# A decoder layer on one core: the first step's way down begun one chunk later, a cast put behind copies, and cached keys asked for ahead of raw weights

## The chip, the cores and the metric

The kernel runs on one core of one Trainium2 chip. The metric is the device time of one execution in microseconds; three runs of the kernel before gave 1118.55 us as their median (1118.25 to 1120.14). The engines are TensorE (PE, matrix products), VectorE (DVE), ScalarE (ACT), GpSimd (POOL) and SyncE (SP), which here issues most of the DMAs. Each engine works through its own queue, and semaphores hold an instruction until what it needs is done.

## The reference

One layer is applied to 576 rows: 512 of a prompt and 8 sample sequences of 8. The width is 1024, the hidden width of an FFN 2816, everything in float32. Cut to what matters:

```
x = x + 0.5 * swiglu(rmsnorm(x), ffn1...)          # silu(x@w_gate) * (x@w_up) @ w_down
h = rmsnorm(x); u_lru, gate, u_pool = split(h @ w_in)
y_lru  = gelu(gate) * rglru(causal_conv(u_lru))     # recurrent branch
y_pool = scale * block_diag(trailing means - u_pool)
x = x + concat(y_lru, y_pool) @ w_out
q = rmsnorm(x) @ wq                                 # cross attention, 4 heads over 256 tokens
x = x + softmax(q @ k.T / 16) @ v @ wo              # k, v from the memory; cached ones for the samples
x = x + 0.5 * swiglu(rmsnorm(x), ffn2...)
y = rmsnorm(x)
```

## The kernel before, in words

Activations are kept transposed, [128 partitions, 8 blocks of the width, 576 rows], and split in two halves of 288 rows (`HT`). Every float32 product is made of three products in a reduced type: each operand is split into a high part (a cast on ACT, L191) and a low part (a subtraction on DVE, L194), and PE multiplies high by high, low by high and high by low (L148). Names in `h` and `l` (`wh_g`, `wl_g`, `dh`, `dl`, `ph`, `pl`) are these parts.

**FFN.** The hidden width is worked through in chunks of 128 columns for gate and up, f = 3 to 21 in this form. A 2 x 2 scheme with seven products instead of eight (the products 11, E, 22, F, G, 12 and H) is used, so weights are summed before they are split: L447 and the adding DMA L450, L465 and L466 on DVE. In the loop `for f in range(plain, FFC)` a chunk runs product 11 (copied to `pa`, L815), E (copied to `e1`, L825), the product 22 of the chunk before (`finish_chunk`, L798), F (copied to `u2`, L846), G, 12, and H; L852, L853, L859, silu L860, L861, L866 and L867 make the hidden values. `u2` must be copied before H overwrites its bank. Raw weights for later chunks are asked for on SP at L433, L440 and L455, and their buffers come free as earlier chunks' splits are done.

**The way down.** The products with w_down are done for groups of four chunks. `quick(g)` puts the 24 steps of group g on a list: for each of four column blocks s11, sE, sF, s12, sH, and sG with s22. After each of a chunk's seven products `fill()` runs one step with `go(1)`. A step multiplies the hidden parts `ph`, `pl` by parts of w_down, `dh` and `dl`; the latter come from loads of `td` on SP (L588), sums on DVE (L606, L608, L609, L617) and a split. `ensure(n)` sees that the first n of these are made. Results are read by copies (`dA`, `dD`, L643, L658) and by `take` (L636: `add`, `add_e`, on ACT, remembered in `taken[0]`) and added to x by adding DMAs on POOL. `build_a` and `build_b` (L556 to L566) sum and split the hidden values of a pair of chunks.

**Cross attention.** `query(p)`, p = 0 to 3, makes two blocks of q with the same seven products. Raw weights `q0_p`, `q1_p` come by SP at L1309 and are summed on POOL (`prepare_q`, L1320 to L1326, for p > 0) and split on ACT and DVE. The keys of the cache, `ck0j` and `ck1j`, come by SP at L1293 (`load_keys`) and are used by `sample_scores` (the products `ss`). Raw weights and keys share the buffers with the tag `wr`, which are handed out in the order of the calls.

**What sets the order.** The order on PE is pinned by the code, product behind product. On ACT, DVE, POOL and SP a scheduler decides the order when the program is built; `after_(a, b)` adds the rule that a comes after b. An engine's order is then fixed.

```
w[q] = ...                                          # parts_of: cast[0] is the last cast, on ACT
taken[0] = s.activation(dst, src, AF.Copy, ...)     # take
after_(silu, taken[0])                              # in the chunk, ahead of H
```

Of the kernel before, what the change touches and what calls it, by code (L numbers as in the profile page):

```python
# [69 lines left out]
def hybrid_step(ctx, tc, a):  # L70
# [70 lines left out]
    def after_(i, j):  # L141

        tc.add_manual_dep(i.ins, j.ins.name, mybir.DependencyInfo(
            mybir.DependencyClass.NoSync, mybir.DependencyReason.DATA), reason="order")
# [223 lines left out]
    def ffn(name, n, fp, turn, plain, head=False):  # L368
# [53 lines left out]
        def parts_of(src, nm_):  # L422
            w = [wp.tile([P, 2, KP, P], F32R, tag=tag, name=f"{tag}_{nm_}") for tag in ("wh", "wl")]
            split(*w, src)
            if out_[0] is not None and nm_ == "e":
                after_(cast[0], out_[0])
            return [lambda q, k, i=i: w[q][:, i, k, :] for i in range(2)]
# [34 lines left out]
        def prepare_g(f):  # L462
            if f < FFC:
                r0, r1 = raws[f]
                v.tensor_add(r0[:, 1], r0[:, 1], r0[:, 0])  # L465
                v.tensor_add(r0[:, 0], r0[:, 1], r1[:, 0])  # L466
                W[f]["G"], W[f]["F"] = parts_of(r0, "g")

        def prepare_h(f):
            if f < FFC:  # L470
# [59 lines left out]
        def go(m):  # L530
            for _ in range(min(m, len(steps))):
                some = steps.popleft()
                for q, *at in some if isinstance(some, list) else [some]:
                    q(*at)
# [254 lines left out]

        before = None  # L790

        def fill():
            go(1)

        def finish_chunk(c):
            w, U, g = c
# [14 lines left out]
        for f in range(plain, FFC):  # L811
            w = W[f]
            U, C, A = (single(tag, f"p{tag}")[:, :HT] for tag in "uca")
            product(U, w["11"], n, N11, True)
            out_[0] = s.copy(A, U)  # L815
            if f == plain:
                if not head:
                    prepare_g(f)
                load_11(f + 2)
            if f == FFC - 5:  # L820
                fetch(0)
            fill()
            product(C, w["E"], n, T1, True)
            e1 = small_tile("e1")
            out_[0] = s.copy(e1, C)  # L825
            prepare_h(f)
            load_12(f + 2)
            if f == plain:
                sum_eh(f + 1)
            if f == 3:  # L830
                build_a(0)
                build_b(0)
            fill()
            if before:
                finish_chunk(before)
                raw[f - 1] = before[2]
                build(f - 1)
            if f == PLAIN[1][0]:
                down(0)
            prepare_e(f + 1)  # L840
            fill()
            if f in range(4, 4 * FAST + 1, 4):
                quick(f // 4 - 1)
            product(U, w["F"], n, T2, False)
            u2 = small_tile("u2")
            out_[0] = s.copy(u2, U)  # L846
            prepare_22(f)
            load_22(f + 2)
            fill()
            product(C, w["G"], n, N22, False)  # L850
            g = full_tile("g")
            v.tensor_add(g[:, HT:], C, u2)  # L852
            v.tensor_mul(g[:, HT:], g[:, HT:], r[:, HT:])  # L853
            sum_eh(f + 2)
            fill()
            if f == plain:
                (n.last if head else n.last_split)(0, ts[0][:, :, 0, :])
            product(A, w["12"], n, N21, False)
            v.tensor_mul(g[:, :HT], A, r[:, :HT])  # L859
            silu = s.activation(g, g, AF.Silu, scale=-1.0)  # L860
            v.tensor_mul(g, g, r)  # L861
            fill()
            if taken[0] is not None:
                after_(silu, taken[0])
            product(U, w["H"], n, T3, False)
            v.tensor_add(e1, U, e1)  # L866
            v.tensor_mul(g[:, HT:], e1, g[:, HT:])  # L867
            if f == plain:
                (n.last if head else n.last_split)(1, ts[1][:, :, 0, :])
            prepare_g(f + 1)  # L870
            load_11(f + 3)
            raw[f] = g
            if f % 2 and f < 4 * FAST:
                build_a(f // 2)
            if f == 3:
                ensure(2)
            fill()
            first[0] = None
            before = w, U, g
# [335 lines left out]
    if True:  # L1215
# [89 lines left out]
        def load_q(p):  # L1305
            if p < KP:
                raws[p] = [wp.tile([P, 2, KP, P], F32, tag="wr", bufs=WRB, name=f"q{i}_{p}") for i in "01"]
                for i, t in enumerate(raws[p]):
                    nc.sync.dma_start(t, a["wqs"][p, :, 2 * i:2 * i + 2])  # L1309
# [22 lines left out]
        def query(p):  # L1332
# [7 lines left out]
                v.tensor_mul(z[:, :, e, p * ST:(p + 1) * ST], q[:, TP:].rearrange("p (b k) -> p b k", k=ST),  # L1340
                             rs.rearrange("p (b k) -> p b k", k=ST))

            load_q(p + 2)
            product(U, w["11"], nx, N11, True)
            s.copy(q0[:, :HT], U)
            product(B, w["H"], nx, T3, True)
# [29 lines left out]
            v.tensor_add(q1[:, :HT], B, q0[:, HT:])  # L1376
            if p:
                sample_scores(2 * p - 2)
            if p < KP - 1:
                load_keys(2 * p + 1)  # L1380
            finish(1, q1)
            if not p:
# [4 lines left out]
            finish(0, q0)  # L1387
            prepare_q(p + 1, "m")
            prepare_q(p + 1, "g")
            if p == 1:  # L1390
                s.activation(nr[:, :1], ones, AF.Exp)

# [335 lines left out]
```

## Time and profile before

| | |
|---|---|
| runs | 1118.55 us median, 1118.25 to 1120.14 |
| the profiled execution | 1118.5 us, of which the span from the first to the last instruction is 1116.6 |
| mean granted clock of TensorE | 0.996 |
| busy: PE, DVE, ACT, POOL | 1102.0, 881.7, 689.0, 212.0 us |
| PE waits for `add` on ACT (L636) | 1.2 us, 2 times |
| PE waits for `u` on ACT (L846) | 1.2 us, once |
| PE waits for keys (`ss`) | 0.9 us, 2 times |
| DVE waits for `td` loads (L608) | 25.9 us, 9 times |

The time of the profiled execution exceeds its span by 1.9 us, which lie outside the instructions. In a row of the timeline the first number is the start in us from the span's start, the second the duration, then engine, line, operation, output and inputs, sizes; brackets at the end give the idle time before it and what ended it. `SPq` rows are SP's DMA issues; `x2` means two, over the time given.

### The profile page before, as it was taken

The numbers are of one execution on the slowest core, as the hardware profiler recorded it, in microseconds if no ns is written. First come the engines' busy times: TensorE is split into PE (matmuls) and PEld (weight loads), VectorE is DVE, ScalarE is ACT, GpSimd is POOL, SyncE is SP. The second block draws the span as 40 slices with busy tenths as digits, with TensorE's granted clock in tenths as the row PEclk, the third lists the DMA queues.
The fourth block names the chain that finished last, engine by engine and source line by source line (L and its number), as shares of the span: only waits on it lengthen the run. The fifth ranks groups of instructions, "written<-read, shape, count | busy, mean of one in ns | idle before, by whom it ended". The sixth has DMA issues, their size and how long they took to land.

```text
span 1116.6 us, 21977 instructions
## 1 busy us (share of the span) xinstructions
PE 1102.0 (99%) x8386; PEld 1082.6 (97%) x8386; DVE 881.7 (79%) x1577; ACT 689.0 (62%) x1293; POOL 212.0 (19%) x247
## 2 busy tenths in 40 slices
PE   9999999999999999999999999999999999999997
PEld 8999999999999999999988879999999999999996
DVE  7899888889865878979865666679888888787754
ACT  8566666665664645786743555456666666666554
POOL 0012222221221034422131000000222222222211
PEclk9999999999999999999999999999999999999998
DMA  9457767776766655577558862243786777777752
GB/s 324 117 132 177 158 156 170 172 169 147 165 140 144 191 154 134 119 216 166 157 184 289 302 210 80 71 104 84 162 184 151 178 177 166 185 160 156 144 111 85
DMA packets 95545, 181.19 MB, mean 162 GB/s; under 512 B 10000, under 2 KB 47888, under 8 KB 95312
## 3 DMA queue, kind: packets, MB, share of 16 engines
q1 hardware_dynamic: 61312, 125.73, 35.4%
q0 software_dynamic: 31472, 51.65, 28.3%
q10 hardware_dynamic: 2656, 2.41, 0.6%
q8 instruction: 65, 1.06, 0.4%
q14 instruction: 40, 0.33, 0.1%
HBM read 141.92 MB, written 13.20 MB: 139 GB/s over the span
## 4 chain that ended last, share of the span: by engine, by line
PE 91%; DMA 3%; DVE 3%; issue 2%; ACT 1%; POOL 0%; POOLq 0%; SPq 0%; DVEq 0%; ACTq 0%
PE pu L148 22%; PE pc L148 10%; PE dU L148 8%; PE pd L148 6%; PE pa L148 5%; PE xo L148 5%; PE wo L148 5%; PE pg L148 4%; PE in_l L148 2%; PE in_p L148 2%; PE in_g L148 2%; PE k L148 2%; PE v L1438 2%; PE dA L148 2%; PE dC L148 2%; PE dD L148 2%
## 5 line engine op out<-in xcount | busy, mean ns | idle before, releaser
L450 POOL DMA_DIRECT2D r<-f_gu x39 | 34.9, 894 | 361.7 <-DVE r L447 197.5
L191 ACT CAST dh<-td 128x512 fp32r<-128x512 f32 x96 | 59.3, 618 | 30.8 <-PE dA L148 10.7
L148 PE MATMUL dU<-ph,dh 128*128 128x288 f32 x256 | 75.7, 296 | 1.2 <-ACT add L636 1.2
L148 PE MATMUL dU<-pl,dh 128*128 128x288 f32 x256 | 75.4, 295 | 0.0
L148 PE MATMUL dU<-ph,dl 128*128 128x288 f32 x256 | 75.4, 295 | 0.0
L194 DVE TENSOR_TENSOR dl<-td,dh 128x512 fp32r<-128x512 f32 x96 | 64.6, 686 | 10.3 <-ACT dh L191 10.2
L194 DVE TENSOR_TENSOR wl_e<-r,wh_e 128x1024 fp32r<-128x1024 f32 x39 | 47.6, 1222 | 28.3 <-ACT wh_e L191 28.3
L652 POOL DMA_DIRECT2D x<-add_e x32 | 38.9, 1214 | 144.6 <-ACT add_e L636 46.8
L191 ACT CAST wh_g<-r 128x1024 fp32r<-128x1024 f32 x39 | 41.0, 1051 | 26.8 <-DVE r L466 13.7
L679 POOL DMA_DIRECT2D x<-add x32 | 31.0, 968 | 136.8 <-ACT add L636 92.5
L194 DVE TENSOR_TENSOR wl_h<-r,wh_h 128x1024 fp32r<-128x1024 f32 x39 | 47.6, 1220 | 3.0 <-ACT wh_h L191 3.0
L148 PEld LDWEIGHTS dU<-ph,dh 128*128 128x128 f32 x256 | 48.1, 188 | 1.6 <-ACT add L636 1.6
L148 PEld LDWEIGHTS dU<-ph,dl 128*128 128x128 f32 x256 | 48.2, 188 | 0.0
L148 PEld LDWEIGHTS dU<-pl,dh 128*128 128x128 f32 x256 | 48.1, 188 | 0.0
L194 DVE TENSOR_TENSOR wl_g<-r,wh_g 128x1024 fp32r<-128x1024 f32 x39 | 47.6, 1222 | 0.3 <-ACT wh_g L191 0.3
L191 ACT CAST wh_h<-r 128x1024 fp32r<-128x1024 f32 x39 | 40.9, 1048 | 10.3 <-PE pu L148 7.2
L191 ACT CAST wh_e<-r 128x1024 fp32r<-128x1024 f32 x39 | 41.1, 1053 | 0.6 <-PE pg L148 0.6
L860 ACT ACTIVATE g<-g 128x576 f32<-128x576 f32 x39 | 26.7, 683 | 23.9 <-DVE g L859 22.3
L686 POOL DMA_DIRECT2D x<-add x32 | 36.9, 1153 | 1.0 <-ACT add L636 0.8
L191 ACT CAST ph<-g 128x576 fp32r<-128x576 f32 (+1 forms) x39 | 22.9, 587 | 18.6 <-DVE g L566 10.5
L825 ACT COPY e<-pc 128x288 f32<-128x288 f32 x39 | 15.6, 401 | 29.1 <-PE pc L148 28.1
L636 ACT ACTIVATE add<-dU 128x288 f32<-128x288 f32 x64 | 26.2, 409 | 11.7 <-PE dU L148 11.7
(649 smaller groups left out, 4650.5 us busy)
## 6 DMA issues: line engine op xcount, KB each, us to landing
x<-add POOLq DMA_DIRECT2D x80, 288.0 KB, 5.7
r<-f_gu SPq DMA_DIRECT2D x39, 512.0 KB, 3.9
r<-f_gu SPq DMA_DIRECT2D x78, 256.0 KB, 3.5
td<-f_d SPq DMA_DIRECT2D x80, 128.0 KB, 4.9
r<-f_gu POOLq DMA_DIRECT2D x39, 256.0 KB, 4.6
x<-add_e POOLq DMA_DIRECT2D x32, 288.0 KB, 4.7
dsum<-f_d POOLq DMA_DIRECT2D x32, 256.0 KB, 4.8
ck<-ck SPq DMA_DIRECT2D x16, 512.0 KB, 4.8
```

Of the source, the lines that this page charges most:

```text
L148: i = te.matmul(*args, **kw)
L191: i = cast[0] = s.copy(hi, src)
L194: return v.tensor_tensor(out=lo, in0=src, in1=f(hi), op=ALU.subtract)
L450: nc.gpsimd.dma_start(r0[:, 0], wgu[f - plain, :, 3], accum_op=ALU.add)
L636: taken[0] = s.activation(dst, src, AF.Copy, scale=0.5 * sign)
L652: nc.gpsimd.dma_start(x[:, j:j + 2, HT:], t, accum_op=ALU.add)
L679: nc.gpsimd.dma_start(x[:, 2 * (i % NQ), :], t, accum_op=ALU.add)
L686: nc.gpsimd.dma_start(x[:, 2 * (i % NQ) + 1, :], t, accum_op=ALU.add)
L825: out_[0] = s.copy(e1, C)
L860: silu = s.activation(g, g, AF.Silu, scale=-1.0)
L1438: te.matmul(ps[:, m, :HD], lhsT=lhs[:, kd, ms], rhs=w[wi][:, k, :], start=kd == 0 and i == 0, stop=kd == DC - 1 and i == 2)
```

## The change

Three edits.

1. In the first FFN (`head`), group 0 of the way down is put on the list at the start of chunk 5, behind product 11, instead of in chunk 4 ahead of F. Its operands for the first two are asked for (`ensure(2)`) in chunk 4 instead of 3. From chunk 6 `fill()` runs two steps instead of one every other time until four extra ones have run, so the 24 steps of group 0 end in chunk 7 as before.
2. In `prepare_g` the cast of the next block's weights (`wh_g`) is put behind the last `take`. This goes for both FFNs.
3. Keys 1 are asked for at the start of query 0, the raw weights of query 2 at its end. Before, the raw weights of query 2 were asked for at the start and keys 1 near the end.

```
@@ prepare_g
                 W[f]["G"], W[f]["F"] = parts_of(r0, "g")
+                if taken[0] is not None:
+                    after_(cast[0], taken[0])
@@ fill and the chunk loop
+        extra = [0]
+
         def fill():
-            go(1)
+            go(1 + extra[0] % 2)
+            extra[0] = max(extra[0] - 1, 0)
...
             out_[0] = s.copy(A, U)
+            if head and f == 5:
+                quick(0)
+            if head and f == 6:
+                extra[0] = 8
...
-            if f in range(4, 4 * FAST + 1, 4):
+            if f in range(8 if head else 4, 4 * FAST + 1, 4):
                 quick(f // 4 - 1)
...
-            if f == 3:
+            if f == (4 if head else 3):
                 ensure(2)
@@ query
-            load_q(p + 2)
+            if p:
+                load_q(p + 2)
+            else:
+                load_keys(1)
...
-            if p < KP - 1:
+            if 0 < p < KP - 1:
                 load_keys(2 * p + 1)
...
             prepare_q(p + 1, "g")
+            if p == 0:
+                load_q(2)
```

Lines of the changed kernel are 2 to 14 higher than those before. The first place is DVE in chunk 4 of the first FFN, from the split of product F's weights on (`td` and `dl` belong to the way down, `pl` to the hidden values, `wl_` to weights). Before:

```order
L194 TENSOR_TENSOR wl_g<-r_582,wh_g 128x1024
L558 TENSOR_TENSOR e<-e,g 128x288
L194 TENSOR_TENSOR pl_752<-t_753,ph_751 128x288
L194 TENSOR_TENSOR dl_764<-td,dh_763 128x512
L194 TENSOR_TENSOR pl_752<-e,ph_751 128x2x288
L606 TENSOR_TENSOR td<-td 128x256
L194 TENSOR_TENSOR wl_h<-r_584,wh_h 128x1024
L194 TENSOR_TENSOR dl_770<-td,dh_769 128x512
L617 TENSOR_TENSOR td<-td 128x256
L798 TENSOR_TENSOR g<-pu,g 128x288
L194 TENSOR_TENSOR wl_e<-r_622,wh_e 128x1024
L196 SCALAR_TENSOR_TENSOR pl_752<-g,ph_751 128x576
```

The same place in the changed kernel, and on to where the first `dl` now stands:

```order
L194 TENSOR_TENSOR wl_e<-r_622,wh_e 128x1024
L196 SCALAR_TENSOR_TENSOR pl_752<-g,ph_751 128x576
L194 TENSOR_TENSOR wl_836<-r_599,wh_835 128x512
L568 TENSOR_TENSOR g<-g,t_753 128x288
L447 TENSOR_TENSOR r_797<-r_749 128x512
L194 TENSOR_TENSOR pl_752<-g,ph_751 128x288
L861 TENSOR_TENSOR g<-pc,u_833 128x288
...
L875 TENSOR_TENSOR e_791<-pu,e_791 128x288
L870 TENSOR_TENSOR g<-g,rstd_n_402 128x576
L466 TENSOR_TENSOR r_622<-r_622,r_642 128x512
L876 TENSOR_TENSOR g<-e_791,g 128x288
L194 TENSOR_TENSOR dl_896<-td,dh_895 128x512
```

The two `dl` and the two sums of `td` have left the place ahead of `wl_e`; the first `dl` stands behind the last instruction that makes chunk 4's hidden values (L876).

The second place is ACT in chunk 11, at the copies of the way down (`add`) and the cast `wh_g` for chunk 12. Before:

```order
L846 COPY u_2417<-pu 128x288
L191 CAST dh_2477<-td 128x512
L636 ACTIVATE add_2431<-dA 128x288
L191 CAST wh_g<-r_2044 128x1024
L636 ACTIVATE add_2460<-dU 128x288
L191 CAST dh_2611<-td 128x512
L636 ACTIVATE add_2431<-dD 128x288
L195 ACTIVATE ph_2521<-g 128x288
L636 ACTIVATE add_2460<-dU 128x288
L860 ACTIVATE g<-g 128x576
```

In the changed kernel:

```order
L855 COPY u_2417<-pu 128x288
L191 CAST dh_2477<-td 128x512
L638 ACTIVATE add_2431<-dA 128x288
L638 ACTIVATE add_2460<-dU 128x288
L191 CAST dh_2611<-td 128x512
L638 ACTIVATE add_2431<-dD 128x288
L195 ACTIVATE ph_2521<-g 128x288
L638 ACTIVATE add_2460<-dU 128x288
L869 ACTIVATE g<-g 128x576
L191 CAST wh_g<-r_2044 128x1024
```

The cast has moved from ahead of three `add` to behind all of them and the silu.

The third place is the query stage on SP and POOL (`q0_2`: first half of the raw weights of query 2). SP in the changed kernel:

```order
L1302 DMA ck01_7075<-ck 128x1024
L1302 DMA ck11_7076<-ck 128x1024
L1318 DMA q0_2_7209<-wqs 128x1024
L1318 DMA q1_2_7210<-wqs 128x1024
L1318 DMA q0_3_7219<-wqs 128x1024
L1318 DMA q1_3_7220<-wqs 128x1024
L1302 DMA ck00_7257<-ck 128x1024
L1302 DMA ck10_7258<-ck 128x1024
```

The first two pairs have changed places; before, `q0_2` and `q1_2` came first. POOL has the same order before and in the changed kernel, here the changed one:

```order
L1335 TENSOR_TENSOR q0_2_7209<-q0_2_7209 128x512
L1329 TENSOR_TENSOR q0_1_6928<-q0_1_6928,q1_1_6929 128x512
L1330 TENSOR_TENSOR q0_1_6928<-q0_1_6928 128x512
L1332 TENSOR_TENSOR q0_1_6928<-q0_1_6928,q1_1_6929 128x512
L1335 TENSOR_TENSOR q0_3_7219<-q0_3_7219 128x512
```

The first add on query 2's weights (L1335, L1326 before) stands ahead of three adds on query 1's (L1329, L1330, L1332; before L1320, L1321, L1323).

## The prediction

> **What bounds the kernel now.** I read the page's busy table and chain first, then the waits of TensorE (PE), then the stretches round each wait.
>
> ```profile
> PE 1102.0 (99%) x8386; PEld 1082.6 (97%) x8386; DVE 881.7 (79%) x1577; ACT 689.0 (62%) x1293; POOL 212.0 (19%) x247
> PE dU L148 <- ACT add L636: 1.2, 2, 0.8
> PE pu L148 <- ACT u L846: 1.2, 1, 1.2
> PE ss L148 <- DMA ck<-ck: 0.9, 2, 0.5
> ```
>
> PE is busy for 99% of the span, and the change neither adds nor takes away a product. So all it can win or lose is idle time of PE, and each of the three edits has one of the waits above beside it: some 3.3 us in all. The other side is as small only if no new wait arises, so the work is to walk each place in the new order with the durations of the old trace. In the rows below the first number is the start in us, the second the duration; from start to start an instruction takes a little less than its duration.
>
> **Part A, the first step's way down.** The stretch round the wait and the two after it (columns: PE, PE loads, DVE, ACT, POOL busy, clock, DMA):
>
> ```profile
> 56.00:74.00 18.00, 16.84 (x127) 16.57 (x126) 17.95 (x34) 11.35 (x22) 2.13 (x2) 1.00 0.44 110
> 74.00:92.00 18.00, 18.00 (x138) 18.00 (x138) 17.85 (x33) 13.05 (x25) 3.80 (x4) 1.00 0.82 198
> 92.00:108.00 16.00, 16.00 (x123) 16.00 (x123) 15.35 (x30) 11.51 (x24) 3.93 (x4) 1.00 0.75 174
> ```
>
> DVE is full from 56 to 92. PE's wait at 70.53 is for the copy `u` on ACT, which stands behind the cast `ph` at 69.75, which waits for the DVE's L566 at 69.26:
>
> ```profile
> 62.81 0.69 DVE L194 TENSOR_TENSOR dl<-td,dh 128x512 fp32r<-128x512 f32 x1
> 63.41 0.76 DVE L194 TENSOR_TENSOR pl<-e,ph 128x576 fp32r<-128x576 f32 x1
> 64.08 0.42 DVE L606 TENSOR_TENSOR td<-td 128x256 f32<-128x256 f32 x1
> 64.42 1.22 DVE L194 TENSOR_TENSOR wl_h<-r,wh_h 128x1024 fp32r<-128x1024 f32 x1
> 65.55 0.69 DVE L194 TENSOR_TENSOR dl<-td,dh 128x512 fp32r<-128x512 f32 x1
> 66.16 0.42 DVE L617 TENSOR_TENSOR td<-td 128x256 f32<-128x256 f32 x1
> 69.26 0.46 DVE L566 TENSOR_TENSOR g<-g,t 128x288 f32<-128x288 f32 x1
> 69.75 0.43 ACT L191 CAST ph<-g 128x288 fp32r<-128x288 f32 x1
> 68.42 0.29 PE L148 MATMUL dU<-ph,dh 128*128 128x288 f32 x1
> 69.08 0.29 PE L148 MATMUL dU<-ph,dl 128*128 128x288 f32 x1
> 70.53 0.40 PE L148 MATMUL pu<-n1h,wh_h 128*128 128x288 f32 x1 [1.16 <-ACT u L846]
> ```
>
> In the new order two `dl` and two `td` leave the queue ahead of L566: by starts 0.60 and 0.61 for the `dl`, 0.34 for each `td`: some 1.88 us. So L566, the cast, the copy and the product H of chunk 4 come 1.88 us earlier: 70.53 - 1.88 = 68.65. But the three steps of the way down that PE ran ahead of H in that chunk leave too. The rows at 68.42 and 69.08 are the first and last of one step: 0.66 us over five intervals, 0.132 us a product, 0.79 us a step of six, 2.38 us for three. PE was ready for H at 69.08 + 0.13 = 69.21, and now is at 66.83. It waits 68.65 - 66.83 = 1.82 us, where it waited 1.32. The wait isn't removed; work that filled part of it is.
>
> Then the first step comes after product 11 of chunk 5. Its third product needs `dl`, which the new order puts behind everything DVE does for the end of chunk 4. In the old order that tail was:
>
> ```profile
> 72.44 0.46 DVE L866 TENSOR_TENSOR e<-pu,e 128x288 f32<-128x288 f32 x1
> 72.81 0.75 DVE L861 TENSOR_TENSOR g<-g,rstd_n 128x576 f32<-128x576 f32 x1
> 73.47 0.69 DVE L465 TENSOR_TENSOR r<-r 128x512 f32<-128x512 f32 x1
> 74.08 0.45 DVE L867 TENSOR_TENSOR g<-e,g 128x288 f32<-128x288 f32 x1
> 74.45 0.69 DVE L466 TENSOR_TENSOR r<-r,r 128x512 f32<-128x512 f32 x1
> ```
>
> L866 came 1.91 us after H's start; so now at 68.65 + 1.91 = 70.56, then L861 (0.66), L466 (0.61), L867 (0.37) and `dl` itself (0.69): about 73.2. H and 11 take 12 products of 0.132 each, 3.17 us together; PE is through at 71.82, runs the first two products of the step, and would want `dl` at 72.08. That is a second wait, of 1.1 us. Part A: 1.82 + 1.1 - 1.32 = **+1.6 us**. The bounds: -1.3 if neither wait arises, +1.9 if `dl` comes 0.3 us later still. I stay at the worked value, since DVE has 0.05 us free in 18 there. The steps that are made up later two at a time (chunks 6 and 7) meet DVE work that is ready; I count no further wait, and the third rival is the case where that fails.
>
> **Part B, the next block's cast behind the takes.** At 190.27 PE waits for `add` on ACT; the same happens at 258.08:
>
> ```profile
> 188.86 1.05 ACT L191 CAST wh_g<-r 128x1024 fp32r<-128x1024 f32 x1 [2.85 <-DVE r L466]
> 189.81 0.40 ACT L636 ACTIVATE add<-dU 128x288 f32<-128x288 f32 x1
> 189.58 0.29 PE L148 MATMUL dD<-ph,dl 128*128 128x288 f32 x1
> 190.27 0.40 PE L148 MATMUL dU<-ph,dh 128*128 128x288 f32 x1 [0.40 <-ACT add L636]
> 257.02 0.29 PE L148 MATMUL dD<-ph,dl 128*128 128x288 f32 x1
> 258.08 0.40 PE L148 MATMUL dU<-ph,dh 128*128 128x288 f32 x1 [0.77 <-ACT add L636]
> 192.44 0.69 ACT L860 ACTIVATE g<-g 128x576 f32<-128x576 f32 x1 [0.66 <-DVE g L859]
> 190.82 1.22 DVE L194 TENSOR_TENSOR wl_g<-r,wh_g 128x1024 fp32r<-128x1024 f32 x1
> 197.52 0.29 PE L148 MATMUL pu<-n1h,wh_g 128*128 128x288 f32 x1
> 178.08 1.75 SPq L588 DMA_DIRECT2D td<-f_d x3
> ```
>
> ACT stood idle for 2.85 us in front of a cast whose source was late, with a ready `add` behind it. With the cast behind the takes, `add` runs as soon as its product is done, and PE's gap goes: 190.27 - 189.58 less a product's 0.13 is 0.56 us, and 258.08 - 257.02 less 0.13 is 0.93. The gain is at most **-1.5 us**. What is late next is `wh_g`: behind the silu it comes at about 193.1 - 0.6, and `wl_g` then ends near 195, against 197.52 - 0.56 = 196.96 for the product that reads it. Also, one chunk earlier `wl_g` (1.2 us) now stands ahead of the two `dl` that release the `td` loads at 178.08, so these land some 1.1 us later, which leaves margins of only 0.5 to 1.5 us there. The bounds are -1.5 and +0.7 (one such margin missed by as much as it now has). I take **-1.4**.
>
> **Part C, keys ahead of raw weights.** The queues in the query stage:
>
> ```profile
> 556.68 1.71 SPq L1293 DMA_DIRECT2D ck<-ck  x2
> q<-wqs SPq DMA_DIRECT2D x4, 512.0 KB, 3.8
> 549.48 1.90 POOL L1326 TENSOR_TENSOR q<-q 128x512 f32<-128x512 f32 x1 [4.86 <-DMA q<-wqs]
> 561.15 1.30 POOL L1320 TENSOR_TENSOR q<-q,q 128x512 f32<-128x512 f32 x1 [9.77 <-DVE wl_qH L194]
> 570.41 0.39 ACT L1345 COPY q<-qu 128x288 f32<-128x288 f32 x1
> 570.85 0.40 PE L148 MATMUL qu<-nxh,wh_qF 128*128 128x288 f32 x1
> 577.85 0.64 PE L148 MATMUL ss<-ck,z_acc 128*32 128x256 f32 x8 [0.39 <-DMA ck<-ck]
> ```
>
> The two pairs of loads swap their turns: the raw weights of query 2 are now issued at 556.68 and land 3.8 us later, at 560.5. POOL's first add on them (L1326) still stands ahead of its adds for query 1 (L1320, L1321). It ran at 549.48, long before; now it starts at about 560.6 and, at 1.3 us (what L1320 took) to 1.9, holds L1320 from 561.15 to between 561.9 and 562.5. From L1320 a chain without slack runs over the casts and splits of query 1 to the copy at 570.41 and to PE at 570.85, which starts as the copy ends. So PE starts 0.75 to 1.35 us later. The wait at 577.85 is for the keys asked for after query 3's weights; those loads stay in their place and move with the rest, so it stays. The bounds are 0 (if the chain had slack I don't see) and +1.35; I take **+1.0**.
>
> That ACT kept its order at 188.86 with a ready instruction behind is a row; for POOL no row shows an instruction held by another's operand. The Trainium skill ("TensorE: Matmul & The Clock Gate", Part 1, the queue depths under "Architectural detail") says that ACT and DVE issue strictly in order and GpSimd's cores too. By that rule part C costs its 1.0 us; were POOL to pass the waiting add, part C would be 0 and the time 1118.7.
>
> **Sum.** Against the profiled execution, 1118.5 us with a span of 1116.6 (0.05 us below the median of the runs, 1118.55): 1118.5 + 1.6 - 1.4 + 1.0 = **1119.7 us**. That is 0.1% more: no change, where 0.2% (2.2 us) is about what a measurement of this kernel can tell.
>
> **Rivals.**
> - *It works as written* (15%). Both waits of part A vanish (-1.3), part B gives -1.5, the keys' wait at 577.85 goes (-0.9 by the table of waits) and POOL holds nothing up: 1118.5 - 3.7 = 1114.8. For it: the three waits are there. Against it: the DVE at 17.95 of 18.00, and the order on POOL.
> - *Nothing of C, the rest as worked* (10%): query 1 has slack, so 1118.7 us.
> - *DVE becomes the bound in chunks 5 to 7* (25%, slower). The 1.88 us of `dl` and `td` work moved out of chunk 4 falls into 74 to 108, where DVE has 0.15 + 0.65 = 0.8 us free. If PE reaches the doubled steps of chunk 6 before their `dl` is split, PE waits for what doesn't fit: 1.88 - 0.8 = 1.1, up to the whole 1.88. That gives 1120.8 to 1121.6. It decides if DVE's split of a step of chunk 6 ends after the step ahead of it. Against it: PE's own waits in part A leave DVE 2.9 us, where before they left 1.3.
> - The forecast (50%) has 1118.5 to 1120.7 as its own range.
>
> So: faster 15%; same 50 + 10 = 60%; slower 25%. The range 1116.2 to 1121.6 holds all but the better half of the first rival and the tail of the third, some 2 in 10.
>
> **What would show it.** Right: in the profile after, PE waits for `u` about 1.8 us near 68.6 and then in the first step of chunk 5 for `dl`; no wait for `add` near 190 and 258; POOL's L1335 (the old L1326) of query 2 starting near 561 plus the shift, just ahead of L1329, and query 1's F late by about 1 us. Wrong: a `u` copy that no longer waits, waits for `wl_g` or `dl` in later chunks, or POOL's add for query 2 behind those for query 1.

## The result and the profile after

The changed kernel takes 1123.0 us, the median of 21 runs (1119.53 to 1125.69); the kernel before takes 1119.49 us in as many runs beside it (1118.11 to 1122.11). The ratio is 1.003, with a 95% interval of 1.0023 to 1.0037: some 3.4 us slower. The prediction said 1119.7 us and no change that can be measured, so it was wrong, and the time lies above its range. The profiled execution of the changed kernel took 1122.82 us with a span of 1120.3, 3.7 us more than the span of before.

The table of waits of the changed kernel (engine, line, what it waits for: us in total, times, longest):

```profile
PE pu L148 <- ACT u L855: 2.5, 3, 1.7
PE ss L148 <- DMA ck<-ck: 1.3, 2, 0.8
PE dU L148 <- DVE dl L194: 0.9, 1, 0.9
PE qu L148 <- ACT q L1357: 0.8, 1, 0.8
PE dU L148 <- ACT add L638: 0.5, 1, 0.5
```

PE waits for `u` three times instead of once, and two lines are new: `dl` and `q`. `add` has gone down from two waits to one, and the two waits for keys (`ss`) take 1.3 us instead of 0.9. Where they lie, from the timeline of PE (start, duration, ..., idle time before it and what ended it):

```profile
68.55 0.40 PE L148 MATMUL pu<-n1h,wh_h 128*128 128x288 f32 x1 [1.67 <-ACT u L855]
73.20 0.40 PE L148 MATMUL dU<-ph,dl 128*128 128x288 f32 x1 [0.94 <-DVE dl L194]
99.90 0.40 PE L148 MATMUL dU<-ph,dh 128*128 128x288 f32 x1 [0.48 <-ACT add L638]
140.41 0.40 PE L148 MATMUL pu<-n1h,wh_h 128*128 128x288 f32 x1 [0.55 <-ACT u L855]
207.69 0.40 PE L148 MATMUL pu<-n1h,wh_h 128*128 128x288 f32 x1 [0.33 <-ACT u L855]
574.00 0.40 PE L148 MATMUL qu<-nxh,wh_qF 128*128 128x288 f32 x1 [0.82 <-ACT q L1357]
```

The bracket leaves out the overlap of two products, about 0.16 us; from start to start, less a product's 0.13, the first five are 1.83, 1.10, 0.64, 0.70 and 0.49 us. The last follows the shorter products `ss`, and is given from start to start: 1.19 us. The first two stand where the prediction put them (68.65 and about 73.2, with 1.82 and 1.1 us). The waits for `add` near 190 and 258 are gone. The last of the six is query 1's F: 0.88 us more than the 0.31 us that the same interval shows in the kernel before. Those at 99.90, 140.41 and 207.69 weren't foreseen.

Where the time went can be read from the starts of the same products in the traces. The table has the time between them in us (the times at its head are those of before: four stretches of the first FFN, then one from the products `ss` ahead of query 1's F into query 2):

| kernel | 58.0 to 123.1 | to 179.9 | to 246.8 | to 287.9 | 569.8 to 582.3 |
|---|---|---|---|---|---|
| before | 65.06 | 56.84 | 66.88 | 41.08 | 12.47 |
| changed | 67.62 | 57.67 | 66.82 | 40.10 | 13.73 |
| changed, another execution | 66.83 | 56.93 | 66.56 | 39.86 | 12.54 |
| edit 1 alone | 67.29 | 58.46 | 67.29 | 40.82 | 12.92 |
| edit 1 alone, again | 66.84 | 58.15 | 67.27 | 40.72 | 12.74 |
| edit 2 alone | 65.03 | 56.84 | 66.77 | 40.10 | 12.12 |
| edit 2 alone, again | 65.04 | 56.84 | 66.48 | 40.95 | 12.14 |
| edit 3 alone | 65.08 | 57.09 | 67.04 | 40.39 | 13.21 |

The chunks of the second FFN take 311.8 to 312.0 us in all of them. The stretch ahead of 58.0 scatters by 1.0 us, the end behind those chunks by 0.5, and the stage of the memory's keys (541 to 570 us) takes 28.8 to 31.9 us whichever edits are in. From 287.9 to 541 edit 2 alone takes 253.6 us in both runs and the others 253.2 to 253.3. So the profiled execution of the changed kernel loses 2.56 us in chunks 4 to 7, 0.83 in the stretch after and 1.26 in the query, and wins 0.06 and 0.98 where edit 2 takes away a wait. Of the 1.26, 0.88 is F and 0.37 the first wait for keys.

### The profile page after: what moved, and what is told of

Its sections match the earlier page's. It is cut to its first block, busy times and chain, and to the rows that moved or that the text cites. A ratio compares the mean times of both kernels' runs of the same rounds, so it can differ in the third digit from the quotient of the medians.

```text
span 1120.3 us, 21937 instructions
## 1 busy us (share of the span) xinstructions
PE 1102.9 (98%) x8386; PEld 1082.6 (97%) x8386; DVE 880.7 (79%) x1577; ACT 687.8 (61%) x1293; POOL 208.8 (19%) x247
## 4 chain that ended last, share of the span: by engine, by line
PE 83%; DVE 8%; DMA 4%; issue 2%; ACT 2%; POOL 1%; SPq 0%; POOLq 0%; DVEq 0%; ACTq 0%
PE pu L148 19%; PE pc L148 9%; PE dU L148 7%; PE pd L148 6%; PE xo L148 5%; PE wo L148 5%; PE pa L148 4%; PE pg L148 4%; PE in_l L148 2%; PE in_p L148 2%; PE in_g L148 2%; PE v L1452 2%; PE dA L148 2%; PE dD L148 2%; PE dC L148 2%
## 5 line engine op out<-in xcount | busy, mean ns | idle before, releaser
L681 POOL DMA_DIRECT2D x<-add x32 | 29.8, 931 | 172.4 <-ACT add L638 138.8
L447 DVE TENSOR_TENSOR r<-r 128x512 f32<-128x512 f32 x39 | 26.8, 688 | 17.0 <-DMA r<-f_gu 17.0
L688 POOL DMA_DIRECT2D x<-add x32 | 35.6, 1112 | 0.2
L870 DVE TENSOR_TENSOR g<-g,rstd_n 128x576 f32<-128x576 f32 x39 | 29.4, 755 | 7.4 <-ACT g L869 7.1
```

What stands on the lines that cost most here:

```text
L447: i = v.tensor_add(r1[:, 1], r0[:, 0], r0[:, 1])
L681: nc.gpsimd.dma_start(x[:, 2 * (i % NQ), :], t, accum_op=ALU.add)
L688: nc.gpsimd.dma_start(x[:, 2 * (i % NQ) + 1, :], t, accum_op=ALU.add)
```

## Experiments

### One edit at a time

Three kernels with one of the edits each, and edit 1 and edit 2 once more in later runs.

> Edit 1 alone (way down of group 0 begun in chunk 5). Theory: it costs the two waits of chunks 4 and 5 and nothing later: 1.8 us for u near 68.6 and 1.1 us for dl near 73.2, against 1.3 before, so +1.6 us; no waits near 99.9 and 140, the old ones near 190 and 258 (0.56 and 0.93 us) still there. Rival: the waits at 99.9 and 140.4 of the changed kernel come from the doubled steps; then they stand here too, 0.6 and 0.7 us, and the edit costs +2.9 us.

> Edit 1 alone once more, on another chip run, to tell its own waits from those of one execution's slow loads. Theory: the waits for u near 69 (1.8), for dl near 74 (1.1) and for add near 126 (0.4) repeat, as DVE is late by its order; the wait for u near 142 (1.16) and those in the stage of the memory keys belonged to slow loads and come out otherwise; the time is +2 to +3 us. Rival: the wait near 142 repeats at 1 us or more: then the edit's own order makes it.

> Edit 2 alone (wh_g behind the takes). Theory: wl_g and the raw load that waits for it come 3 to 4 us later in every chunk, so DVE's L447 waits for that load and the cast ph ahead of u is late: the waits for add near 190 and 258 go (-1.5 us) and waits for u come near 140 and 207 (0.7 and 0.5 us): about -0.3 us in all, with DVE's wait L447 for its load near 17 us instead of 4.8. Rival: those new waits are the other edits' doing, and edit 2 alone is worth -1.5 us.

> Edit 2 alone, again. If its gain is real (0.9991 with an interval that just reaches 1), the ratio is 0.999 again, and the waits for add near 190 and 258 are gone. If it was luck, 1.000 or more.

> Edit 3 alone (keys 1 ahead of the raw weights of query 2). Theory: POOL's first add of query 2 stands waiting ahead of the adds of query 1, so query 1's F starts 0.9 us late, and the keys asked for later land 0.4 us later still against their use: +1.2 us in all. Rival: the query stage has slack and the edit alone is 0 (the changed kernel's delay there would come from what FFN 1 left behind).

| kernel | us, median | before | ratio, 95% interval | us |
|---|---|---|---|---|
| edit 1 | 1122.35 | 1118.86 | 1.0027, 1.0017 to 1.0037 | +1.9 to +4.1 |
| edit 1 again | 1122.13 | 1118.64 | 1.0036, 1.0023 to 1.0048 | +2.6 to +5.4 |
| edit 2 | 1118.22 | 1118.86 | 0.9991, 0.9981 to 1.0001 | -2.1 to +0.1 |
| edit 2 again | 1118.52 | 1118.85 | 0.9995, 0.9986 to 1.0004 | -1.6 to +0.4 |
| edit 3 | 1120.01 | 1118.86 | 1.0005, 0.9995 to 1.0016 | -0.6 to +1.8 |

The last column is the interval times 1118.9 us. Edit 1 is the one that costs: 3 to 4 us, where the prediction had 1.6. Edit 2 gains about 0.8 us (the mean of the two) and edit 3 costs about 0.6, but these three intervals hold 0. Together that makes +3 to +4, so the times agree with edits that add up.

In edit 1 alone the waits of chunks 4 and 5 are the same (1.83 and 1.10 us in both runs), and a third one follows in chunk 8:

```profile
141.66 0.40 PE L148 MATMUL pu<-n1h,wh_h 128*128 128x288 f32 x1 [1.00 <-ACT u L853]
```

The first profiled execution of edit 1 is the slowest of its eight runs. In the second run it is

```profile
140.53 0.40 PE L148 MATMUL pu<-n1h,wh_h 128*128 128x288 f32 x1 [0.91 <-ACT u L853]
```

that is 1.16 and 1.07 us from start to start. The kernel before has no wait there. The two waits for `add` of edit 2's places, 0.56 and 0.93 us before, are 0.89 and 0.96 (0.87 in the second run).

### Is it the doubled steps?

The prediction's third rival blamed the steps that are made up two at a time. This kernel has edit 1 without them:

```
-            if head and f == 6:
-                extra[0] = 8
```

> Edit 1 alone, but fill() always runs one step, so the last three steps of group 0 end in chunk 8, just before group 1 is put on the list. Theory: the waits for u in chunk 4 (1.8 us) and for dl in chunk 5 (1.1 us) are there all the same; the wait for u in chunk 8 near 141 (1.07 and 1.16 us in two looks), which the doubled steps of chunk 6 make by bunching the adding DMAs of group 0 against the loads of group 1, goes: +1.6 to +2 us against before. Rival: that wait stays at about 1 us, and the cause is that everything behind chunk 5 is late: +3 us.

1121.91 us against 1119.66: 1.0015 (1.0003 to 1.0027). The interval overlaps that of edit 1, so the time doesn't decide. In the trace the wait for `u` near 140 has gone, and one of 1.24 us stands at 137.55, of another product for another operand:

```profile
PE dC L148 <- DVE pl L194: 1.1, 1, 1.1
PE pu L148 <- ACT u L851: 1.7, 1, 1.7
```

It is another wait: DVE works without a gap from 131.72 up to it and waits for no `td` load there. So this kernel doesn't show what makes the wait for `u`. The changed kernel shows more: its second execution below has the doubled steps and no wait in chunks 6 to 8. They don't make one by themselves.

### Chunk 4: what stands ahead of `u`

Three attempts at the first two waits. In the first, the operands are asked for as early as before (`if f == 3: ensure(2)`), with the first step still in chunk 5.

> Edit 1 alone, but the operands of the first two steps are still made in chunk 3 and 4 as before (ensure(2) at f = 3), so two dl and two td sums stand ahead of L566 on DVE again. Theory: DVE's work up to H and the first step is the bound: the wait for dl goes, and the wait for u grows by the 1.88 us that L566 is later, to 3.7 us less what the step no longer waits: sum 2.9 to 3.7 us, no gain over edit 1 alone (+3 us). Rival: only the late dl costs, the wait for u stays at 1.8 and the sum falls to 1.8 us.

1.0045 (1.003 to 1.0059), no better than edit 1 alone. The wait for `dl` has gone, and that for `u` has grown by 1.57 us:

```profile
70.66 0.40 PE L148 MATMUL pu<-n1h,wh_h 128*128 128x288 f32 x1 [3.24 <-ACT u L853]
```

3.40 us in one place instead of 1.83 + 1.10 = 2.93 in two. DVE's work between 56 and 73 has to be done either way; here its place decided mainly which product waits. A third wait, 0.89 us for `u` in chunk 8, is there too.

In the second, on top of all three edits, DVE's last difference and split of a pair (L566 and the cast `ph` behind it) are put behind the copy of `u` in the program's text; it was run twice.

```
-            v.tensor_sub(b21, b21, t2[p])
-            split(hi[:, T4, :], lo[:, T4, :], b21)
+            def rest(): ...            # the same two, called behind u2's copy
+            if head and p:
+                late_b.append(rest)
```

> The changed kernel, and in FFN 1 the last difference and split of build_b (L568 and the cast ph behind it) is put behind the copy u. Theory: in chunk 4 DVE is the bound, so the wait of 1.8 us for u goes, H runs at about 66.8, and the step's wait for dl grows from 1.1 to 2.9 us: no gain there; the waits for u near 140, 207 and 275 (0.70, 0.50, 0.25 us) go: -1.4 us against the changed kernel, +2 us against before. Rival: ACT's order is the bound in chunk 4 too, dl stays at 1.1 us, and the gain is 1.8 + 1.4 = 3.2 us: no slower than before.

> The changed kernel with u first once more: its first profile was taken in the fastest of its runs (1119.12 us, median 1121.4). Theory: the waits of chunk 4 and 5 (1.58 and 1.25 us) repeat, and no wait for u near 140 and 207 comes, so FFN 1 up to 288 us keeps most of the 2.7 us it was shorter than in the changed kernel. Rival: the waits near 100 and 140 are back and that first look was luck.

1121.4 us, 1.0025 (1.0012 to 1.0038): inside the changed kernel's interval. The waits are 1.58 and 1.25 us (1.59 and 1.26 in the second execution, which took 1124.17 us), 2.83 together. That second execution also has waits near 125 and 140 (0.38 and 0.48 us) that the first has not. The copy of `u`:

```profile
67.76 0.40 ACT L864 COPY u<-pu 128x288 f32<-128x288 f32 x1 [2.16 <-DVE g L572]
```

L572 is the difference itself. It reads `t2`, and `t2`, `e1` and `u2` share two buffers, so the copy still waits for it; only the cast `ph` has changed places. The copy starts 0.35 us earlier than in the changed kernel, and PE's wait is 0.25 us shorter. That ACT stood behind the cast `ph` was thus only a small part of the reason. Edit 2 with the same thing came to 0.9989 (0.9973 to 1.0004), no different from edit 2 alone; its trace has a wait for `add` of 1.70 us at 191.6:

> Edit 2 alone, with build_b's last difference and split put behind the copy u in program order (as in the run of all three edits with u first). Theory: edit 2's gain near 190 and 258 stays and its new waits near 205 and 272 (0.41 and 0.25 us) go: -1.5 us against before, the best version. Rival: they stay, or chunk 4 gets worse, and it is no better than edit 2 alone (-1.0 us).

In the third, two low splits of weights on DVE (`wl_e` and the one for product 22) are put behind L566, with all three edits and with edit 2 alone:

```
-            split(*w, src)
+            low = split(*w, src)
+            if head and bsub[0] is not None and nm_ in ("e", "22"):
+                after_(low, bsub[0])
```

> The changed kernel, and in FFN 1 DVE's low splits of the next block (wl_e, wl of 22) come behind build_b's difference (L568), on which u's buffer waits. The first dl now stands ahead of L568 too. Theory: it is the order on DVE, not its amount of work, that makes the two waits of chunks 4 and 5: u waits about 1.6 us instead of 1.8, dl no longer (1.1 us less), and the waits for u near 140 and 207 (0.7 and 0.5 us) shrink to under 0.2: some 2.5 us better than the changed kernel, +1 us against before. Rival: DVE's amount of work is the bound from 56 to 92, so the two waits keep their sum of 2.9 us in another split, and it is +2 to +2.5 us.

> Edit 2 alone with the order on DVE of the first run of this group (low splits of the next block behind build_b's difference). Theory: edit 2's gain near 190 and 258 (1.5 us) stays and its waits for u near 205 and 272 (0.41 and 0.25 us) go: -1.6 us against before, the best version. Rival: the low splits that are put off make E of the next chunk wait, and it is no better than edit 2 alone (-1.0 us).

1132.2 us (1.0133, 1.0112 to 1.0153) and 1130.8 us (1.0112, 1.0098 to 1.0126): the rule moved much more than the two splits in the schedule. In chunks 4 and 5 the first of them has one wait, 2.15 us for `u`, and none for `dl`: 0.8 us less than the two of the changed kernel, so the order on DVE and not only its amount of work had a part in them. But the later chunks wait for `add`, with the edits

```profile
PE dU L148 <- ACT add L642: 5.4, 3, 3.2
```

and without:

```profile
PE dU L148 <- ACT add L642: 6.2, 6, 2.1
```

Such a rule costs far more than it wins.

### The third wait: a load that lands behind an add

In edit 1 alone, `u` of chunk 8 is late because DVE is. Here are DVE and POOL ahead of that wait, in the second run of edit 1:

```profile
126.73 0.89 POOL L679 DMA_DIRECT2D x<-add  x1 [4.74 <-ACT add L636]
127.31 1.22 POOL L686 DMA_DIRECT2D x<-add  x1
135.47 0.43 DVE L608 TENSOR_TENSOR td<-td 128x256 f32<-128x256 f32 x1 [1.95 <-DMA td<-f_d]
139.26 0.46 DVE L566 TENSOR_TENSOR g<-g,t 128x288 f32<-128x288 f32 x1
```

And in the kernel before:

```profile
125.12 1.21 POOL L686 DMA_DIRECT2D x<-add  x1
131.32 0.43 DVE L608 TENSOR_TENSOR td<-td 128x256 f32<-128x256 f32 x1 [0.26 <-DMA td<-f_d]
135.10 0.45 DVE L566 TENSOR_TENSOR g<-g,t 128x288 f32<-128x288 f32 x1
```

DVE waits 1.95 us (2.27 in the first run) for a load of `td`, where it waited 0.26. The first try was to take away one adding DMA ahead of it, `add_e` of column 3 (L652, issued at 120.78, in the kernel before at 116.54):

```
-                nc.gpsimd.dma_start(x[:, j:j + 2, HT:], t, accum_op=ALU.add)
+                if not (head and i == 3):
+                    nc.gpsimd.dma_start(x[:, j:j + 2, HT:], t, accum_op=ALU.add)
```

> Edit 1 alone, and the adding DMA of add_e for the last column block of group 0 (288 KB, issued at 120.78 us, 4.2 us later than before) is left out, so the result lacks that part of the first FFN; nothing else moves on any queue. Theory: this DMA slows the loads behind it and, through L455 and the loads of td, makes DVE late in chunk 8: without it the td load there takes 5.4 us instead of 7.1, and the wait of 1.1 us for u near 140.5 goes. Rival: the wait stays at 1 us; the lateness comes from before, not from that DMA.

1120.96 us, 1.0018 (1.0005 to 1.0032). The wait for `u` in chunk 8 is gone, DVE waits less:

```profile
134.46 0.43 DVE L608 TENSOR_TENSOR td<-td 128x256 f32<-128x256 f32 x1 [0.74 <-DMA td<-f_d]
```

That points to the adding DMAs; which one was still open. The next kernel was to test the order of two neighbours on POOL; nothing else moves in it.

```
-                nc.gpsimd.dma_start(r0[:, 0], wgu[f - plain, :, 3], accum_op=ALU.add)
+                d = nc.gpsimd.dma_start(r0[:, 0], wgu[f - plain, :, 3], accum_op=ALU.add)
+                if head and xadd and f == 8:
+                    after_(d, xadd[-1][1])     # behind the last add to x
```

> Edit 1 alone, with one pair of neighbours on POOL put back as it stood before: the adding DMA L450 of the raw weights (113.08 in edit 1 alone, behind an idle time of 5.21 us) now stands behind the two adding DMAs of x of column 2. Nothing else moves on any engine. If POOL's order is what brings the wait for u in chunk 8 (1.16 and 1.07 us near 141), that wait goes, as it does where the adding DMA of column 3 is left out, and the ratio falls from 1.003 to about 1.002. If the order is harmless because the adds themselves are ready only at about 113.3 (ACT's last add of that column ends there, against 109.4 before), the x adds move by less than 1 us, DVE still waits about 2 us for the td load of chunk 8 and PE still about 1 us for u, and the ratio stays at 1.003: then the late column, not the order on POOL, is the cause.

1.0027 (1.0016 to 1.0038), with 1.15 us for `u` at 140.4: as edit 1. But the pair moved was that of column 1, not of column 2 as the expectation says, so for the pair that was meant it shows nothing. A kernel with edits 1 and 3 everywhere and edit 2 in the second FFN only went with it:

```
-                if taken[0] is not None:
+                if taken[0] is not None and not head:
```

> Edits 1 and 3, with edit 2 in the second FFN alone. The changed kernel's raw loads (L433) of the first FFN are issued later by edit 1 (126.88 against 124.41 us for chunk 8) and by edit 2 on top of it (130.87), and in three places its DVE or ACT then waits. If edit 2's late wh_g is what uses up that lead in the first FFN, the waits at 99.9 and 207.7 go, those for add near 194 and 262 come back, and the runs scatter less; the time is then that of edits 1 and 3 alone, 1.003 to 1.004, if edit 2 gains 1.0 in the first FFN whatever the loads do; below 1.003 if its gain is used up by the loads there.

1124.05 us, 1.0044 (1.003 to 1.0058); the changed kernel has 1.0023 to 1.0037. By the mark that it set (below 1.003) the first of the two expectations holds: the waits at 99.9 and 207.7 are gone, and those for `add` are back, 1.07 us at 193.39 and 0.79 at 261.09. The two intervals overlap, so that edit 2 still gains in the first FFN beside edit 1 is likely and not shown. Its profile gave the hint for the third wait, since it hasn't one near 140. Yet in the first FFN every engine and queue of this kernel has the same order as with edit 1 alone. So the third wait isn't fixed by that order: two profiled executions with it have the wait, and this one, the fastest of its five runs, has not. The DMA view of single issues, in windows of 0.1 us (size, us from issue to landing), has in the second run of edit 1, for the second `x` add (127.31) and the second of the three `td` loads (128.26):

```profile
x<-add POOLq DMA_DIRECT2D x1, 288.0 KB, 7.9
td<-f_d SPq DMA_DIRECT2D x1, 128.0 KB, 7.1
```

127.31 + 7.9 = 135.2 and 128.26 + 7.1 = 135.4: the load lands right behind the add. In the kernel before (add at 125.12, load at 125.80):

```profile
x<-add POOLq DMA_DIRECT2D x1, 288.0 KB, 7.9
td<-f_d SPq DMA_DIRECT2D x1, 128.0 KB, 5.4
```

133.0 and 131.2: the load lands ahead of it. In the four profiles with edit 1 and no edit 2 that have the late load (both runs of edit 1, early operands, the moved neighbours), it is issued 0.95 to 1.13 us after the add and lands about 0.2 us after it; in the kernel before it is 0.68 us, in the kernel with edit 2 left out of the first FFN 0.23 us, and the load lands ahead of the add. With edit 3 alone it is 0.65 us; the load lands ahead there too, but takes 6.6 us, and DVE waits 1.40 us without a wait of PE. Where `add_e` was left out, the load still landed behind the add, but the add itself was done in 6.7 us, and the load in 5.9. The last kernel therefore moves that one add of edit 1 alone behind the next adding DMA on POOL; nothing else moves on any engine.

```
-                nc.gpsimd.dma_start(x[:, 2 * (i % NQ) + 1, :], t, accum_op=ALU.add)
+                if head and i == 3:
+                    late_x.append(put_x)       # issued behind L450 of chunk 10
+                else:
+                    put_x()
```

> Edit 1 alone, with the second adding DMA of x of column 3 (L686, issued at 127.31 in edit 1 alone) put behind the adding DMA of the raw weights that follows it on POOL (L450, 133.5); nothing else moves on any engine. In edit 1 alone the second td load of chunk 8 is issued 0.95 to 1.13 us after that x add and lands about 0.2 us after it (135.38 against 135.19), 7.1 us after its issue; in the kernel before it is issued 0.68 us after it and lands before it, after 5.4 us. If the td load waits its turn behind the x add, it now takes 5.0 to 5.5 us, DVE waits under 0.5 us for it (1.95 before), the wait for u near 140.5 goes, and the ratio falls to about 1.002 (the two waits of chunks 4 and 5, 1.6 us net). If the load is late for another reason, DVE's 2 us and PE's 1 us near 140.5 stay, and the ratio is 1.003 to 1.004 as for edit 1 alone.

The `td` load in the DMA view, then the timeline of POOL and DVE, then the table of waits:

```profile
td<-f_d SPq DMA_DIRECT2D x1, 128.0 KB, 5.5
```

```profile
133.55 0.89 POOL L450 DMA_DIRECT2D r<-f_gu  x1 [6.23 <-DVE pl L194]
133.91 0.42 DVE L610 TENSOR_TENSOR td<-td 128x256 f32<-128x256 f32 x1 [0.35 <-DMA td<-f_d]
134.10 1.23 POOL L689 DMA_DIRECT2D x<-add  x1
```

```profile
PE pu L148 <- ACT u L860: 1.7, 1, 1.7
```

The load takes 5.5 us instead of 7.1, DVE waits 0.35 instead of 1.95, and PE waits for `u` once, in chunk 4. The time is 1121.06 us, 1.0023 (1.0011 to 1.0034); by itself that interval doesn't part from edit 1's, the trace does. With the profiles above it makes the late load the cause of the third wait in edit 1 alone; by itself one execution would not, since the run with edit 2 left out of the first FFN, in edit 1's own order, went without the wait too. What is left is the 1.6 us of chunks 4 and 5 and 0.6 us by which the waits for `add` are larger (0.45, 1.00 and 0.66 us, against 0.56 and 0.93 before).

### The changed kernel's own late waits

In the changed kernel POOL and SP stand in another order than with edit 1 alone. One more execution of it:

> The changed kernel once more, to tell waits of its order from those of one execution. Theory: the waits near 68.6 (1.8), 73.2 (1.1), 140 (0.7) and 574 (1.2) repeat within 0.2 us; those near 100 (0.64) and for the keys near 581 (0.9) depend on when loads land and come out otherwise. Rival: all repeat.

This execution took 1119.09 us, and of the six waits only those at 68, 73 and 572 are there (1.83, 1.11 and 1.16 us). It is 0.6 us from the prediction's time, in part by luck: the table has +1.9 us for edit 1's two stretches and -1.5 for edit 2's, close to the prediction, but 0.07 for the query, where the waits for keys shrank by about as much as F was late. The profiled one took 1122.82. What differs in chunks 6 and 8 are loads of raw weights (L433). One issued at 90.5 takes, in the profiled execution and in the other:

```profile
r<-f_gu SPq DMA_DIRECT2D x1, 512.0 KB, 6.1
```

```profile
r<-f_gu SPq DMA_DIRECT2D x1, 512.0 KB, 5.2
```

and DVE behind it waits 1.85 us in the one and 0.93 in the other (timeline of DVE, one row of each):

```profile
96.64 0.69 DVE L447 TENSOR_TENSOR r<-r 128x512 f32<-128x512 f32 x1 [1.85 <-DMA r<-f_gu]
```

```profile
95.47 0.69 DVE L447 TENSOR_TENSOR r<-r 128x512 f32<-128x512 f32 x1 [0.93 <-DMA r<-f_gu]
```

Behind it come L803 on DVE (L798 before), `ph` on ACT and the copy for which PE waits at 99.90; in the two executions that copy stands at

```profile
99.46 0.39 ACT L638 ACTIVATE add<-dU 128x288 f32<-128x288 f32 x1
```

```profile
98.29 0.39 ACT L638 ACTIVATE add<-dU 128x288 f32<-128x288 f32 x1
```

For chunk 8 SP issues that load at 130.87 in the changed kernel, at 126.88 with edit 1 alone and at 124.41 before:

```profile
130.87 0.33 SPq L433 DMA_DIRECT2D r<-f_gu  x1
```

```profile
126.88 0.33 SPq L433 DMA_DIRECT2D r<-f_gu  x1
```

```profile
124.41 0.33 SPq L433 DMA_DIRECT2D r<-f_gu  x1
```

It takes 6.4 us in the profiled execution and 5.4 in the other. The wait at 207.69 isn't traced to a load: the one asked for at 198.7 takes 5.6 us, and 5.7 in the other execution. What the lost lead does shows in DVE's waits, in the table of waits of the kernel before, of edit 2 alone, and of the changed kernel:

```profile
DVE r L447 <- DMA r<-f_gu: 4.8, 4, 1.8
```

```profile
DVE r L447 <- DMA r<-f_gu: 15.1, 12, 2.0
```

```profile
DVE r L447 <- DMA r<-f_gu: 17.0, 15, 2.0
```

With edit 2 alone, `wl_g` comes 2.0 to 4.5 us later in three of every four chunks from the fourth on, so its raw buffer comes free later and the next load is asked for later. DVE now waits for it 12 to 15 times instead of 4. By itself that costs PE little (0.41 us near 205 and 0.25 near 272 in edit 2 alone, 0.74 near 272 in its second run), but it leaves a load that is 1 us slower nothing to hide behind. Most runs of the changed kernel lie nearer 1123 than 1119, so the profiled execution is the common case. That the time goes with these loads is read from two executions only, and why a load takes longer in the one is open.

### Keys and raw weights: POOL's order

With edit 3 alone, POOL in the query stage:

```profile
560.15 1.83 POOL L1326 TENSOR_TENSOR q<-q 128x512 f32<-128x512 f32 x1 [15.78 <-DMA q<-wqs]
561.94 1.28 POOL L1320 TENSOR_TENSOR q<-q,q 128x512 f32<-128x512 f32 x1
571.48 0.40 PE L148 MATMUL qu<-nxh,wh_qF 128*128 128x288 f32 x1 [0.81 <-ACT q L1348]
```

The first add on query 2's weights waits for its load and stands ahead of query 1's adds, as foreseen. This kernel puts it behind them:

```
+                    if p == 2:
+                        after_(i, fadd[1])     # behind query 1's adds for F
```

> Edit 3 alone, with POOL's first add of query 2 put behind query 1's adds of F. Theory: the queue on POOL is the whole delay of query 1's F: its wait for the copy (0.9 us more than before) goes, and the time is that of before within 0.4 us; keys 1 asked for earlier gain nothing. Rival: the delay comes from the loads (the raw weights land later), and F is still 0.9 us late.

```profile
564.20 1.30 POOL L1320 TENSOR_TENSOR q<-q,q 128x512 f32<-128x512 f32 x1 [18.04 <-DVE wl_qH L194]
567.08 1.29 POOL L1326 TENSOR_TENSOR q<-q 128x512 f32<-128x512 f32 x1
574.02 0.40 PE L148 MATMUL qu<-nxh,wh_qF 128*128 128x288 f32 x1
```

Query 1's F now starts without a bracket (0.44 us from start to start instead of 1.19). The order on POOL is the cause of F's wait in edit 3. The time is 1118.95 us, 1.0005 (0.9994 to 1.0015): no gain over the kernel before either, since the waits for the keys (`ss`) are still there, 0.62 and 0.52 us by the bracket against 0.39 and 0.50 before.

No version is shown to beat the kernel before: edit 2 comes nearest, and all three of its intervals, alone and with `u` first, hold 1.

## Why the prediction was wrong

- **Part A, the two waits: right.** 1.83 us at 68.55 (worked: 1.82 at 68.65) and 1.10 at 73.20 (worked: 1.1). The terms listed for `dl` add up to 72.9; with L866's own 0.37 us, which the list leaves out, they make the 73.2. The bottleneck there is DVE, as the kernel with early operands shows: the two waits became one of 3.40. DVE's order has a part in it: with two splits put off it was one of 2.15. The reason given for `u`, that ACT stands behind the cast `ph`, was a small part; the copy waits for L566 directly, through the shared buffer.
- **Part A, "I count no further wait": this step failed.** It looked at the doubled steps and found their operands ready, and no wait for `dl` came there. The cost came from what the step's results trigger: the adds to `x` and the loads of `td` and raw weights move too, each by its own amount. With edit 1 alone, an add and a load that were 0.68 us apart came to be 0.95 to 1.13 us apart, the load landed behind the add, and 1.1 us of PE's time were lost in chunk 8. With all edits the wait there is for a raw load and smaller (0.70), with 0.64 at 99.9; those two come in one execution and not in the other. Edit 1 was priced +1.6 and measured +3 to +4. In the stretches of the profiled execution it is +3.4, which is 1.8 of the 2.4 us by which the forecast fell short there; 0.4 are edit 2's and 0.3 the query's.
- **The third rival: right sign, wrong mechanism.** 1120.8 to 1121.6 was too low by 1.4 us at least, and DVE as the bound of the doubled steps isn't what happened: PE never waits for `dl` in chunks 6 and 7, one execution with doubled steps has no wait in chunks 6 to 8, and with edit 1 alone the wait in chunk 8 follows a late load.
- **Part B: mechanism right, size uncertain.** Both waits go. -1.4 was worked out; the stretches give -1.0 and -1.5 in the changed kernel's two executions and -1.1 and -0.5 in those of edit 2 alone, whose times give -1.0 and -0.6 with intervals that hold 0. What is missing, up to 0.9 us, lies mostly with new waits for `u` (0.25 to 0.74 us). The prediction put 0.1 us on late loads and named those of `td`; the ones that DVE came to wait for more often are those of L433, behind `wl_g`.
- **Part C: the wait right, its price not shown.** POOL's L1335 stands at 562.78, ahead of L1329 at 564.47, and F of query 1 lost 0.88 us, within 0.75 to 1.35. The query stretch lost 1.26, 0.07 and, with edit 3 alone, 0.74 us, since the waits for keys behind F change too; they did not stay as the prediction had it. Edit 3 alone costs 0.6 us, with an interval that holds 0. The prediction's alternative, that POOL passes a waiting add, would not have changed this: L1335 was already running when the last operand of L1329, the split `wl_qH`, was done at 563.35.

```profile
562.12 1.23 DVE L194 TENSOR_TENSOR wl_qH<-q,wh_qH 128x1024 fp32r<-128x1024 f32 x1 [2.11 <-ACT wh_qH L191]
562.78 1.73 POOL L1335 TENSOR_TENSOR q<-q 128x512 f32<-128x512 f32 x1 [15.88 <-DMA q<-wqs]
564.47 1.28 POOL L1329 TENSOR_TENSOR q<-q,q 128x512 f32<-128x512 f32 x1
```

## What to carry to other kernels

When a step is moved, list what its results set off (adds to memory, buffers that come free, loads that are then asked for) and write down for each of these how far it is from its neighbours in the DMA queues before and after; a wait that isn't near the moved work was a third of edit 1's cost here. Moving work out of the way of a product that waits for a full engine can move the wait and not remove it: count what that engine must do up to the next product that needs it. And where an edit takes the lead from loads, read the trace of more than one execution: here margins of less than 1 us held in some and failed in others.

## What the hardware showed

- A load of 128 KB on SP's queue took 5.4 to 6.6 us when issued 0.65 to 0.68 us behind a 288 KB adding DMA on POOL's queue, landing ahead of it, and 7.0 to 7.4 us when issued 0.95 to 1.13 us behind it, landing just after the add; with the add moved away it took 5.5. The Trainium skill ("DMA: Bandwidth & Descriptors", "Issuing engines are not separate DMA queues") says that transfers issued from different engines run on the same 16 DMA engines and interleave. These runs agree with that: the load's time changes with an add that another engine issued.
- With edit 3 alone an add on POOL whose operand was done at 560.83 us started at 561.94, because the add ahead of it in the queue had started at 560.15 and took 1.83 us; with the two turned round F's interval falls from 1.19 to 0.44 us. The Trainium skill ("TensorE: Matmul & The Clock Gate", Part 1, "Architectural detail") has GpSimd's cores in strict order. No run here tests that: the add ahead was running, and no longer waiting for its load, when the other became ready.
- The same load of 512 KB, issued at the same place of the same kernel, took 5.2 us in one execution and 6.1 in another.
